# First output projection of a two-layer trunk: tokens stationary, seven block products for five of eleven row-tile pairs, result turned on TensorE

## The chip, the cores and the metric

The kernel runs on one core of a Trainium2 chip. The time is the device time of one execution in microseconds (us); of the kernel before, three runs gave 965.71, 966.10 and 966.26 us, median 966.1. A profile is one execution recorded by the hardware profiler. The engines are named as in the profile: PE is TensorE (matrix products; PEld its loads of stationary operands), DVE VectorE, ACT ScalarE, POOL GpSimd, SP the queue that issues the loads.

## The reference

The reference computes a decoder trunk in float32 for 256 tokens of width 1024. There are two layers; the first mixes tokens with a short convolution, the second with sparse attention. The part that the change touches is the first half-step feed-forward block and the start of the convolution mixer:

```python
def swiglu_ffn(x, w_in, w_out):
    gate, up = jnp.split(x @ w_in, 2, axis=-1)
    return (jax.nn.silu(gate) * up) @ w_out
...
    h = h + 0.5 * swiglu_ffn(rmsnorm(h, ffn1_norm[i]), ffn1_w_in[i], ffn1_w_out[i])
    hn = rmsnorm(h, mix_norm[i])
    h = h + short_conv_mixer(hn, conv_w_in[i], conv_w[i], conv_w_out[i])
```

The inner width is 2816, that is 22 tiles of 128 (`NF`). `short_conv_mixer` projects to three parts b, c and v, forms u = c v, runs a causal convolution of three taps over the tokens, multiplies with b and projects again.

## The kernel before, in words

**Numbers in two parts.** Each float32 operand is split into a high part in a shorter format (`F32R`) and the low rest. A product of tokens x and weights w is the sum of three: xh wh, xl wh and xh wl. ScalarE casts the high part of the weights (`Stream.high`, line 238), VectorE subtracts to get the low part (`Stream.low`, line 266). A weight unit is 128x1024 elements, eight tiles of 128x128, and half of a loaded chunk of 1 MB.

**Usual layout.** The residual h lies feature-major: eight tiles h[c] of 128 features x 256 tokens. Weights are stationary on TensorE, tokens move: [xh | xl] as 512 columns against wh, xh as 256 columns against wl (`half` and `a_pass`, lines 429 to 439). The order of the two passes alternates.

**The input projection** (`ffn_in`) makes the 22 inner tiles one after the other, two PSUM banks each; `ffn_evac` normalises by R, applies the gate and splits the result.

**The first output projection** (`out_proj`) makes eight output tiles c; each is a sum over 22 inner tiles, 44 matmuls. `out_evac` adds half of the result to h[c] and at once makes the next norm's operands for this tile: a high and a low part of g h[c] (`Norm.tile`, lines 379 and 383), and the squares on GpSimd. The norm factor R itself (`Norm.rows`) is a product with a matrix of ones, a square root and a reciprocal. It is not needed by the matmuls that follow, only by the evacuation of their results.

**The convolution's input projection** has eight groups f. Each takes three weight units (for c, v and b) into a pair of banks (`ocv`, a buffer of two) and one more bank, 24 matmuls of 512 and 24 of 256 columns. In group f=0, R is made between the sixth and the last k-tile (`conv_mid`). `conv_evac` then works through ScalarE, VectorE and GpSimd: sum of the two passes (lines 448, 449), product c v and its factor R squared on GpSimd (730, 731), taps (739 to 741), product with b (743) and a split (442, 443). Between its steps up to three weight units of later groups are prepared. Its output feeds the convolution's output projection, which starts with three output tiles over the first seven of the eight inputs.

**The last output projection** (`out_pairs`, matmuls at lines 1412 and 1464) is written differently. Tokens are stationary there (128 tokens, two halves) and weights move, 512 columns at a time. Inner tiles go in pairs p. A plain pair takes eight products of blocks; a block pair takes seven, in the manner of Strassen and Winograd, with sums of weight blocks that VectorE makes in place (line 167) and sums of token blocks made by `Pairs.add`. The set `PLAIN` says which pairs are plain. `add_pairs` puts the parts of the weights in an order: beside pair p, the second half of pair p+1 and the first parts of a block pair p+2. The parts of each go into eight PSUM accumulators, m[1] to m[8], from which sums give the four quarters of the result.

**What sets the order.** Every engine runs its instructions in the order in which the program writes them. There is no planner here, except a hand-written order for the attention, which is not touched. A wait of one instruction holds all behind it on its engine.

## Time and profile before

| What | Before |
|---|---|
| median of three runs | 966.1 us |
| span of the profiled execution | 963.8 us |
| first output projection (130.05 to 191.14) | 61.09 us |
| convolution's input projection (191.14 to 258.06) | 66.9 us |
| last output projection (903.47 to 960.56) | 57.1 us |

No time of the profiled execution as a whole is given beside its span; the span runs from its first to its last instruction. A row of the chain of waits has a start, a length, an engine, what it writes, its line and a count of merged instructions. A row of the timeline has the engine before the line; in square brackets stands how long the engine was idle before it and whose result ended that. A row of instruction groups has busy time and mean ns of one behind the bar.

### The profile page before, as it was taken

How to read it: one execution, taken by the hardware profiler on the slowest of the kernel's cores; microseconds unless marked ns; L12 is line 12 of the kernel's file. 1: busy time of each engine (PE TensorE's matmuls, PEld its weight loads, DVE VectorE, ACT ScalarE, POOL GpSimd, SP SyncE). 2: the span in 40 equal slices, each digit the busy share in tenths (PEclk: the TensorE clock that was granted, in tenths of full speed). 3: DMA queues.
4: the chain of work that ended last, by engine and by line, in shares of the span. 5: the costliest groups of instructions: out<-in, count | busy, mean ns of one | idle time of the engine just before them, and what ended most of it. 6: DMA issues, size and time to landing. Idle time of an engine off the chain costs nothing.

```text
span 963.8 us, 14683 instructions
## 1 busy us (share of the span) xinstructions
PE 958.1 (99%) x5609; PEld 839.4 (87%) x5609; DVE 755.0 (78%) x1213; ACT 581.9 (60%) x982; POOL 174.2 (18%) x266
## 2 busy tenths in 40 slices
PE   9999999999999999999999999999999999999998
PEld 7888888888888888888888888888987888888887
DVE  7987776678889888767659787866688788879896
ACT  7665653455556665644548787743479656656553
POOL 1000001144470100011321031001337350000002
PEclk9999999999999999999999999999999999999999
DMA  8665555546546975555635657554620364467362
GB/s 299 227 216 177 189 204 179 183 167 209 187 137 223 272 238 181 183 211 179 214 131 178 202 193 259 175 183 175 219 89 1 129 221 142 164 217 248 118 205 88
DMA packets 36423, 178.61 MB, mean 185 GB/s; under 512 B 3424, under 2 KB 7152, under 8 KB 18560
## 3 DMA queue, kind: packets, MB, share of 16 engines
q1 hardware_dynamic: 36352, 177.67, 54.1%
q8 instruction: 44, 0.72, 0.3%
q14 instruction: 27, 0.22, 0.1%
HBM read 175.52 MB, written 1.08 MB: 183 GB/s over the span
## 4 chain that ended last, share of the span: by engine, by line
PE 97%; DVE 1%; POOL 1%; DMA 0%; ACT 0%; issue 0%; SPq 0%; POOLq 0%
PE mm L430 55%; PE a L430 26%; PE a L1412 4%; PE mm L1412 2%; PE mm L1177 1%; PE a L1242 1%; PE a L812 1%; PE a L813 1%; PE a L814 1%; PE mm L655 1%; PE a L1222 1%; PE a L694 1%; DMA base<-in_first_dram 0%; POOL pr L1214 0%; DVE pr L1185 0%; PE a L925 0%
## 5 line engine op out<-in xcount | busy, mean ns | idle before, releaser
L266 DVE TENSOR_TENSOR wl<-ws,wh 128x1024 fp32r<-128x1024 f32 x263 | 326.5, 1252 | 68.4 <-ACT wh L238 42.8
L430 PE MATMUL mm<-xs,wh 128*128 128x512 f32 x1480 | 348.8, 390 | 0.0
L430 PEld LDWEIGHTS mm<-xs,wh 128*128 128x128 f32 x1480 | 273.6, 188 | 54.5 <-DVE xs L383 0.2
L238 ACT CAST wh<-ws 128x1024 fp32r<-128x1024 f32 x263 | 272.2, 1046 | 35.8 <-PE a L430 21.1
L430 PEld LDWEIGHTS mm<-xs,wl 128*128 128x128 f32 x1480 | 185.2, 192 | 4.2
L430 PE MATMUL mm<-xs,wl 128*128 128x256 f32 x1480 | 187.4, 283 | 0.0
L430 PE MATMUL a<-act,wh 128*128 128x512 f32 x608 | 141.7, 390 | 0.0
L430 PEld LDWEIGHTS a<-act,wh 128*128 128x128 f32 x608 | 113.0, 188 | 22.7
L449 DVE TENSOR_TENSOR t<-mm,t 128x512 f32<-128x512 f32 x95 | 65.2, 686 | 60.6 <-ACT t L448 59.9
L448 ACT COPY t<-mm 128x512 f32<-128x512 f32 x95 | 55.6, 585 | 73.7 <-PE mm L430 73.3
L430 PEld LDWEIGHTS a<-act,wl 128*128 128x128 f32 x608 | 75.7, 191 | 1.6
L430 PE MATMUL a<-act,wl 128*128 128x256 f32 x608 | 76.4, 283 | 0.0
L473 ACT ACTIVATE t<-t 128x256 f32<-128x256 f32 x88 | 36.8, 418 | 57.1 <-DVE t L460 57.0
L379 ACT ACTIVATE xs<-base 128x256 fp32r<-128x256 f32 x48 | 24.1, 506 | 77.0 <-DVE base L573 62.1
L460 DVE TENSOR_TENSOR t<-t,R 128x512 f32<-128x512 f32 (+1 forms) x88 | 57.3, 651 | 2.6
L442 ACT CAST act<-t 128x256 fp32r<-128x256 f32 x91 | 37.0, 407 | 28.8 <-DVE t L743 18.2
L397 POOL TENSOR_TENSOR t<-base 128x256 f32<-128x256 f32 x35 | 26.3, 751 | 134.7 <-DVE base L573 108.5
L443 DVE TENSOR_TENSOR act<-t,act 128x256 fp32r<-128x256 f32 x91 | 38.6, 424 | 5.7 <-ACT act L442 5.7
L383 DVE SCALAR_TENSOR_TENSOR xs<-base,xs 128x256 fp32r<-128x256 f32 x48 | 29.7, 622 | 16.9 <-ACT xs L379 16.8
L394 POOL TENSOR_TENSOR sq<-base 128x256 f32<-128x256 f32 x5 | 3.1, 615 | 219.4 <-DVE base L573 211.0
L474 DVE TENSOR_TENSOR t<-t,t 128x256 f32<-128x256 f32 x88 | 36.8, 418 | 4.6 <-ACT t L473 4.6
L1437 POOL TENSOR_TENSOR t<-t,base 128x512 f32<-128x512 f32 x4 | 5.9, 1478 | 163.6 <-ACT t L1435 163.6
(318 smaller groups left out, 1148.5 us busy)
## 6 DMA issues: line engine op xcount, KB each, us to landing
ws<-in_ffn_w_in_dram SPq DMA_DIRECT2D x69, 1024.0 KB, 5.0
ws<-in_ffn_w_out_dram SPq DMA_DIRECT2D x33, 1024.0 KB, 4.8
ws<-in_conv_w_in_dram SPq DMA_DIRECT2D x12, 1024.0 KB, 4.8
base<-in_ffn_w_in_dram SPq DMA_DIRECT2D x11, 1024.0 KB, 5.3
ws<-in_w_kv_dram SPq DMA_DIRECT2D x6, 1024.0 KB, 4.9
base<-in_ffn_w_pairs_dram SPq DMA_DIRECT2D x12, 512.0 KB, 4.7
kt<-in_ffn_w_in_dram SPq DMA_DIRECT2D x5, 1024.0 KB, 7.9
ws<-in_conv_w_out_dram SPq DMA_DIRECT2D x4, 1024.0 KB, 5.0
```

Of the source, the lines that this page charges most:

```text
L238: ac.copy(h, src)
L266: ve.tensor_tensor(out=l, in0=src, in1=h.bitcast(F32), op=ALU.subtract)
L383: ve.scalar_tensor_tensor(out=xs[c][:, T:], in0=h[c], scalar=gt[:, g + c:g + c + 1], in1=xs[c][:, :T].bitcast(F32), op0=ALU.mult, op1=ALU. ...
L430: pe.matmul(o if x == 0 else o[:, :T], u[x][:, q * P:(q + 1) * P], rhs if x == 0 else rhs[:, :T], start=start, stop=stop, skip_group_check ...
L442: ac.copy(dst[:, :T], src)
L443: ve.tensor_tensor(out=dst[:, T:], in0=src, in1=dst[:, :T].bitcast(F32), op=ALU.subtract)
L448: ac.copy(r, o[:, :, T:])
L449: ve.tensor_tensor(out=r, in0=o[:, :, :T], in1=r, op=ALU.add)
L460: ve.tensor_tensor(out=r, in0=r, in1=R[:, None, :].to_broadcast([P, n, T]), op=ALU.mult)
L473: ac.activation(s, r[:, 0], AF.Silu)
L474: ve.tensor_tensor(out=s, in0=s, in1=r[:, 1], op=ALU.mult)
L1412: pe.matmul(m[n], x, w, start=(count[n] == 0 and i == 0), stop=(count[n] == total[n] - 1 and i == 2), skip_group_check=True)
```

## The change

The first output projection now takes the form of the last one: tokens stationary, six plain pairs (0, 2, 5, 8, 9, 10) and five block pairs (`PLAIN1`). The weight array of the first layer is rearranged in memory for this, by the same function as that of the last. The layout of h must stay feature-major. So each of the four quarters of the result (`11`, `21`, `12`, `22`: token half, feature half), scaled by 0.5 R, is turned by four 128x128 transposes on TensorE, and VectorE adds the turned quarter to h (`turned`). The norm's operands are made by quarters (`piece`), and the squares by quarters of four tiles (`square4`). The factor 0.5 R is needed as a column per token; two small matmuls make it during the input projection (`half_rows`). Group f=0 of the convolution is cut in pieces (`conv_first`): k-tiles 0 to 3 of its first unit, then the turn of the last quarter, then k-tiles 0 to 3 of the other two units, then k-tiles 4 to 7 of all three. R is made in group f=1. A load of a small table moves from the end of the convolution into the input projection.

```diff
+    PLAIN1 = (0, 2, 5, 8, 9, 10)
...
-    W.add(A["ffn1_w_out"][0])
+    SEC1 = W.add_pairs(A["ffn1_w_pairs"], second_home, PLAIN1)
+    W.other.update({SEC1.c0 + p: (1, "kt", 0)[p % 3] for p in range(NP)})
...
+        def piece(self, c, at):
+            v = slice(T + at.start, T + at.stop)
+            for xs, g in self.sets:
+                ac.activation(xs[c][:, at], h[c][:, at], AF.Copy, scale=gt[:, g + c:g + c + 1])
+                ve.scalar_tensor_tensor(out=xs[c][:, v], in0=h[c][:, at], scalar=gt[:, g + c:g + c + 1], in1=xs[c][:, at].bitcast(F32),
+                                        op0=ALU.mult, op1=ALU.subtract)
+
+        def square4(self, x, tt):
+            s, to = act((P, 4, P), F32), self.sq[:, tt * P:(tt + 1) * P]
+            ac.activation(s, kt8[:, 4 * x:4 * x + 4, tt * P:(tt + 1) * P], AF.Square)
+            po.tensor_tensor(out=s[:, :2], in0=s[:, :2], in1=s[:, 2:], op=ALU.add)
...
+    def half_rows(R):
+        pb, r = bank(), sm([P, 2])
+        for tt in range(2):
+            pe.matmul(pb[:, tt:tt + 1], R[:1, tt * P:tt * P + P], ones[:1, :1], start=True, stop=True)
+        ac.activation(r, pb[:, :2], AF.Copy, scale=0.5)
+        return r
...
+        def turned(name, x, tt):
+            pb = bank([P, 4, P])
+            for a in range(4):
+                pe.transpose(pb[:, a], s[name][:, a * P:(a + 1) * P], ident)
+            v = kt8[:, 4 * x:4 * x + 4, tt * P:(tt + 1) * P]
+            ve.tensor_tensor(out=v, in0=pb, in1=v, op=ALU.add)
+
+        for p in range(last + 1):
+            B.product(p, *(2, 4 if p else 8) if p in S.plain else (1, 2))
+            B.prepare(p)
+            B.product(p, *(8, 4, 3) if p in S.plain else (3, 7, 6, 5, 4) if 0 < p < last else (1, 6, 7, 5, 2, 3, 4))
+        p = last + 1
+        B.product(p, 2, 4)
+        B.prepare(p)
+        s["s1"] = t2()
+        ac.copy(s["s1"], m[1])
+        B.product(p, 3, 8)
+        B.prepare(p + 1)
...
+        rest = range(p + 1, NP)
+        W.high()
+        W.low()
+        for q in rest:
+            B.product(q, 2)
+        add(s["11"], 2, s["11"], 0)
+        W.high()
+        W.low()
+        for q in rest:
+            B.product(q, 4)
+        add(s["21"], 4, s["21"], 1)
+        turned("11", 0, 0)
+        norm.square4(0, 0)
+        for n, q in enumerate(rest):
+            if n == len(rest) - 1:
+                turned("21", 0, 1)
+            B.product(q, 3)
+        for c in range(4):
+            norm.piece(c, slice(0, T))
+            if c == 1:
+                add(s["12"], 3, s["12"], 0)
+        for n, q in enumerate(rest):
+            if n == len(rest) - 1:
+                turned("12", 1, 0)
+            B.product(q, 8)
+        for c in range(4, 8):
+            norm.piece(c, slice(0, P))
+        norm.square4(0, 1)
+        add(s["22"], 8, s["22"], 1)
+        W.close(S)
+
+        def end():
+            turned("22", 1, 1)
+            for c in range(4, 8):
+                norm.piece(c, slice(P, T))
+            norm.square4(1, 0)
+            norm.square4(1, 1)
+            norm.ends()
...
+    def conv_first(end):
+        ob, ocv = bank(), bank2()
+        turn[0] = 0
+        o = [ocv[:, 0], ocv[:, 1], ob]
+        us = W.take(2)
+        a_pass([(o[0], us[0], xs, range(4))])
+        end()
+        a_pass([(o[1], us[1], xs, range(4))])
+        us += W.take(1)
+        a_pass([(o[2], us[2], xs, range(4))])
+        a_pass([(a, u, xs, range(4, 8)) for a, u in zip(o, us)])
+        W.done(3, False)
+        X["conv"] = conv_evac(0, ocv, ob, zs)
+        next(X["conv"])
+        W.pump()
...
-    for f in range(8):
+    for f in range(1, 8):
         ob, ocv = bank(), bank2()
-        a_group([ocv[:, 0], ocv[:, 1], ob], xs, mid=conv_mid if f == 0 else None, fresh=f < 2)
-        weave(conv_evac(f, ocv, ob, *box[0], zs), 1 if f == 7 else 3)
+        a_group([ocv[:, 0], ocv[:, 1], ob], xs, mid=conv_mid if f == 1 else None, fresh=f < 2)
+        if f == 1:
+            weave(X.pop("conv"), 2)
+        weave(conv_evac(f, ocv, ob, zs), 1 if f == 7 else 3)
```

The order of the instructions shows three places. The first is ScalarE of the changed kernel, at the end of f=0 of the convolution: L424 and L430 are the pieces and squares of the last quarter, `wh_1932` is the third weight unit of f=0, L482 the copy of f=0's first two banks, and the casts behind it are the three units of f=1.

```order
L424 ACTIVATE xs_1410<-base 128x128 [waits DVE_49]
L424 ACTIVATE xs_1411<-base 128x128
L424 ACTIVATE xs_1412<-base 128x128
L424 ACTIVATE xs_1413<-base 128x128
L430 ACTIVATE act_1911<-base 128x512
L430 ACTIVATE act_1916<-base 128x512
L243 CAST wh_1932<-ws_1745 128x1024 [waits DMAHW4_49,PE_49]
L482 COPY t_343_1968<-mm_1888 128x512 [waits PE_49,Activation_49]
L243 CAST wh_1971<-ws_1745 128x1024
L243 CAST wh_1977<-ws_1802 128x1024 [waits DMAHW5_49]
L243 CAST wh_1981<-ws_1802 128x1024
```

The units of f=0 and f=1 are cast here behind the pieces, where before they came ahead of the end of the projection.

The second place is VectorE around the reciprocal R. In the kernel before (L412 the reciprocal, L449 the sum of a group's banks, L266 a weight's low part, L443 the end of an evacuation), f=0's evacuation and then f=1's sum:

```order
L412 RECIPROCAL R_1948<-t_318_1946 128x256 [waits Activation_49]
L449 TENSOR_TENSOR t_321_1958<-mm_1900,t_321_1958 128x512 [waits Activation_49]
L266 TENSOR_TENSOR wl_1963<-ws_1859,wh_1961 128x1024 [waits DMAHW2_49,Activation_49]
L734 TENSOR_TENSOR t_325_1969<-a_1899,t_325_1969 128x256 [waits Activation_49]
L266 TENSOR_TENSOR wl_1977<-ws_1859,wh_1973 128x1024 [waits Activation_49]
L740 SCALAR_TENSOR_TENSOR t_329_1979<-u_1965,base,t_329_1979 128x256 [waits Activation_49]
L741 SCALAR_TENSOR_TENSOR t_329_1979<-u_1965,base,t_329_1979 128x256 [waits DVE_49]
L266 TENSOR_TENSOR wl_1985<-ws_1895,wh_1983 128x1024 [waits DMAHW3_49,Activation_49]
L743 TENSOR_TENSOR t_329_1979<-t_329_1979,t_325_1969 128x256 [waits DVE_49,Pool_49]
L443 TENSOR_TENSOR act_1988<-t_329_1979,act_1988 128x256 [waits Activation_49]
L449 TENSOR_TENSOR t_335_2041<-mm_1992,t_335_2041 128x512 [waits Activation_49]
```

And in the changed kernel, where the reciprocal stands in f=1 (L446 the reciprocal, L271 a low part, L477 the end of an evacuation, L483 the sum of f=1's banks):

```order
L446 RECIPROCAL R_2050<-t_362_2048 128x256 [waits Activation_49]
L901 TENSOR_TENSOR t_366_2064<-a_1887,t_366_2064 128x256 [waits PE_49,Activation_49]
L271 TENSOR_TENSOR wl_2072<-ws_1983,wh_2068 128x1024 [waits PE_49,Activation_49]
L907 SCALAR_TENSOR_TENSOR t_370_2074<-u_2060,base,t_370_2074 128x256 [waits Activation_49]
L908 SCALAR_TENSOR_TENSOR t_370_2074<-u_2060,base,t_370_2074 128x256 [waits DVE_49]
L271 TENSOR_TENSOR wl_2080<-ws_1993,wh_2078 128x1024 [waits DMAHW0_49,PE_49,Activation_49]
L910 TENSOR_TENSOR t_370_2074<-t_370_2074,t_366_2064 128x256 [waits DVE_49,Pool_49]
L477 TENSOR_TENSOR act_2083<-t_370_2074,act_2083 128x256 [waits Activation_49]
L271 TENSOR_TENSOR wl_2090<-ws_1993,wh_2086 128x1024 [waits PE_49,Activation_49]
L483 TENSOR_TENSOR t_377_2092<-mm_2002,t_377_2092 128x512 [waits Activation_49]
```

Evacuation 0 now follows f=1's group on TensorE, a third low part stands ahead of f=1's sum, and evacuation 1, further down, has no low parts between its steps.

The third place is VectorE at the end of the changed projection (L811 sums out of PSUM, L822 a turned quarter added to h, L425 the low pieces of the norm's operands):

```order
L811 SCALAR_TENSOR_TENSOR t_324_1779<-mm_1419,sm_403,t_324_1779 128x512 [waits Activation_49]
L271 TENSOR_TENSOR wl_1785<-ws_1708,wh_1783 128x1024 [waits DMAHW3_49,Activation_49]
L811 SCALAR_TENSOR_TENSOR t_321_1772<-a_1416,sm_403,t_321_1772 128x512 [waits PE_49]
L271 TENSOR_TENSOR wl_1804<-ws_1708,wh_1800 128x1024 [waits Activation_49]
L811 SCALAR_TENSOR_TENSOR t_323_1777<-a_1417,sm_403,t_323_1777 128x512 [waits PE_49]
L822 TENSOR_TENSOR base<-a_1819,base 128x4x128 [waits PE_49]
L822 TENSOR_TENSOR base<-a_1835,base 128x4x128 [waits PE_49]
L425 SCALAR_TENSOR_TENSOR xs_1406<-base,xs_1406 128x256 [waits Activation_49]
L425 SCALAR_TENSOR_TENSOR xs_1407<-base,xs_1407 128x256 [waits Activation_49]
L811 SCALAR_TENSOR_TENSOR t_322_1775<-a_1418,sm_403,t_322_1775 128x512 [waits PE_49]
```

None of these rows stands there before; the sums of the quarters, the lows of the convolution's weights and the pieces take turns in one queue.

More of the change, by code (lines that the diff above doesn't have):

```diff
@@ L247, in low @@
             half = self.half.pop(0)
-            if len(half) == 6 and not isinstance(half, list):
+            if len(half) == 7:
                 self.pair_low(*half)
@@ L357, in tables @@
     def tables():
-        sy.dma_start(small, A["small"])
         row = t2()
@@ L1370, in residual @@
         if f == 2:
-            pb, X["rows"] = bank(), sm([P, 2])
-            for tt in range(2):
-                pe.matmul(pb[:, tt:tt + 1], hid.R[:1, tt * P:tt * P + P], ones[:1, :1], start=True, stop=True)
-            ac.activation(X["rows"], pb[:, :2], AF.Copy, scale=0.5)
+            X["rows"] = half_rows(hid.R)
         if f in TURNS:
```

176 lines of the change are left out of this document (126 added, 50 removed).

## The prediction

> **What bounds the kernel now.** I read the page first, then the chain of waits, then single stretches.
>
> ```profile
> span 963.8 us, 14683 instructions
> PE 958.1 (99%) x5609; PEld 839.4 (87%) x5609; DVE 755.0 (78%) x1213; ACT 581.9 (60%) x982; POOL 174.2 (18%) x266
> PE 97%; DVE 1%; POOL 1%; DMA 0%; ACT 0%; issue 0%; SPq 0%; POOLq 0%
> ```
>
> TensorE is busy for 99% of the span and carries 97% of the chain: every TensorE microsecond saved counts, and so does every one in which TensorE is made to wait. The chain in order of time gives the stages:
>
> ```profile
> 24.46 105.59 PE mm L430 x608
> 130.05 61.09 PE a L430 x352
> ...
> 199.75 3.64 PE mm L430 x16
> ...
> 249.75 3.63 PE mm L430 x16
> ...
> 257.10 23.23 PE a L430 x136
> ...
> 575.50 0.87 PE a L895 x8
> ...
> 797.15 0.53 PE a L1373 x4
> 797.69 105.79 PE mm L430 x608
> 903.47 1.36 PE a L1412 x6
> ...
> 913.08 3.43 PE a L1412 x15
> ...
> 957.68 2.88 PE a L1464 x24
> ```
>
> The first output projection is the row at 130.05: 352 matmuls, 61.09 us, no gap. The same algebra that the change brings runs already as the last projection (L1412, L1464), from 903.47 to 960.56, also without a gap. At 199.75 ends f=0 of the convolution, with R made in it, and f=1 begins. The L1412 row of fifteen matmuls gives 3.43 / 15 = 0.2287 us for a matmul of 512 columns. Other engines have room on average, not everywhere:
>
> ```profile
> 903.47:957.68 54.21, 54.21 (x240) 44.51 (x239) 48.03 (x54) 29.93 (x36) 5.88 (x4) 1.00 0.43 141
> 130.05:191.14 61.09, 61.09 (x354) 54.14 (x353) 37.69 (x48) 27.69 (x33) 9.27 (x13) 1.00 0.54 190
> ```
>
> (Columns: stretch, length, then busy PE, PEld, DVE, ACT, POOL, clock, DMA.) VectorE works 48.03 of 54.21 us in the last projection and 37.69 of 61.09 in the first.
>
> **The change, TensorE's share.** The order of the new kernel has 249 matmuls of 512 columns in the section (six plain pairs of 24, five of 21): 249 x 0.2287 = 56.9 us for 61.09, a saving of 4.2. It adds sixteen 128x128 transposes; the row at 575.50 has eight in 0.87 us, so 1.75. The half-step column costs the row at 797.15, 0.53. Building the pair operands beside the input projection costs 105.79 - 105.59 = 0.2 by the two rows with 608 matmuls. Sum: -4.2 + 1.75 + 0.53 + 0.2 = **-1.7 us**, if nothing waits.
>
> **VectorE in the section.** The last projection shows the pace at which weights become ready:
>
> ```profile
> 908.09 2.36 DVE L172 TENSOR_TENSOR wl<-kt,wh 128x1024 fp32r<-128x1024 f32 x2 [0.53 <-ACT wh L161]
> 910.37 2.35 DVE L172 TENSOR_TENSOR wl<-ws,wh 128x1024 fp32r<-128x1024 f32 x2
> ...
> 914.38 2.67 DVE L167 TENSOR_TENSOR base<-base 128x1024 f32<-128x1024 f32 x3
> 917.52 2.36 DVE L172 TENSOR_TENSOR wl<-base,wh 128x1024 fp32r<-128x1024 f32 x2 [0.47 <-ACT wh L161]
> ...
> 947.51 2.35 DVE L172 TENSOR_TENSOR wl<-kt,wh 128x1024 fp32r<-128x1024 f32 x2
> 949.78 0.68 DVE L1429 SCALAR_TENSOR_TENSOR t<-mm,t 128x512 f32<-128x512 f32 x1
> base<-in_ffn_w_pairs_dram SPq DMA_DIRECT2D x12, 512.0 KB, 4.7
> ```
>
> VectorE runs there almost without a break: 1.15 us for a low part, 0.62 for a half one, 2.6 for the three subtractions (L167) of a block pair and 0.5 until ScalarE's cast is back. Count from the section's start. The lows of pair 1 are done at 910.45 - 903.47 = 6.98. The order of the new kernel prepares, beside each pair, the second half of the next one and the first one and a half parts of a block pair after it. Beside pair 1 these are three lows and a half one: 3.97, so 10.95. Beside pair 2, subtractions and two lows of block pair 3 and one and a half of block pair 4: 2.6 + 4 lows' worth less a half, 6.65, so 17.6 (the cast that waits for the chunk finds it landed, 4.7 and an issue behind 6.98). Beside pair 3, subtractions, a turn-around and two lows of pair 4: 5.4, so 23.0. Then 4.0 (27.0), 6.65 (33.65), 5.35 (39.0), 2.3 (41.3) and 2.3 (43.6). In the last projection block and plain pairs alternate up to 7 and 8; here two block pairs in a row come twice, 3, 4 and 6, 7, and eat the lead. Block pair 7 starts on TensorE at 35.67 (three plain pairs of 5.49, four block pairs of 4.80) and wants its third part at 37.5; its low is there at 37.95: a wait of 0.45, which goes into the tail's sum below and not beside it, because VectorE sets both. The last chunk's load is issued at 39.0, when the lows of pair 7 free its buffer; it lands 5.1 later (4.7 plus the first half's issue, 0.4), two casts of about 1.0 and one low of 1.2 behind them follow: 47.45.
>
> **The turned tail.** From 47.45 VectorE owes, before the last quarter can be turned: eight sums out of PSUM (0.68 to 0.75, 5.8 together), two convolution lows (2.4), three turned quarters added to h (0.69, 2.1), four full pieces of the low half (0.48, 1.95), four half pieces, and some 1.6 of waits for ScalarE (three turn-arounds of 0.5). Rows:
>
> ```profile
> L449 DVE TENSOR_TENSOR t<-mm,t 128x512 f32<-128x512 f32 x95 | 65.2, 686 | 60.6 <-ACT t L448 59.9
> L448 ACT COPY t<-mm 128x512 f32<-128x512 f32 x95 | 55.6, 585 | 73.7 <-PE mm L430 73.3
> L238 ACT CAST wh<-ws 128x1024 fp32r<-128x1024 f32 x263 | 272.2, 1046 | 35.8 <-PE a L430 21.1
> 193.06 0.48 DVE L383 SCALAR_TENSOR_TENSOR xs<-base,xs 128x256 fp32r<-128x256 f32 x1 [0.58 <-ACT xs L379]
> L521 DVE TENSOR_TENSOR t<-t,t 128x128 f32<-128x128 f32 x15 | 4.3, 286 | 0.2
> L1196 ACT ACTIVATE pr<-pr,sm 128x128 f32<-128x128 f32 x32 | 12.6, 403 | 0.0
> ```
>
> A half piece is not in the trace: 0.29 (L521) to 0.48 (L383) on VectorE, I take 0.30; on ScalarE 0.40 alone (L1196), 0.33 in a row. Sum 15.05, so the last turn may begin at 62.5 and ends at 63.05. TensorE by itself would be there at 56.9 + 4 x 0.44 + 1.39 (four of the convolution's k-tiles) = 60.05. TensorE's four turns stand in its queue between the last products, so that whatever a turn waits for holds the products behind it too. **Wait 3.0**, bounds 0.5 (VectorE's turn-arounds hidden) to 5 (one load late by its own 4.7).
>
> **The third convolution unit.** ScalarE's order puts the cast of f=0's third weight unit (wh_1932 in the order shown ahead) behind everything that the last quarter releases; the unit's source has long landed. From the end of the turn: VectorE's add 0.75, four half pieces 1.3, two squares 1.05 (585 ns each, overlapping), the cast 1.05: 4.15. TensorE has one k-half of the second unit, 1.39. It waits 2.75, and then 0.35 more for the low part (1.2 against four matmuls, 0.9): **3.1**, bounds 2.5 to 3.6. Next, the casts for f=1 stand behind the copy of f=0's banks, which are full four matmuls (0.91) before f=0 ends: 0.59 + 1.05 - 0.91 = **0.75**, bounds 0.3 and 1.2.
>
> **The convolution's chain.** R is now made in f=1's group, not f=0's: every evacuation needs it. Rows of the evacuations:
>
> ```profile
> 199.24 1.75 DVE L412 RECIPROCAL R<-t 128x256 f32<-128x256 f32 x1 [4.01 <-ACT t L410]
> ...
> 208.50 0.42 DVE L443 TENSOR_TENSOR act<-t,act 128x256 fp32r<-128x256 f32 x1 [0.47 <-ACT act L442]
> 208.98 0.69 DVE L449 TENSOR_TENSOR t<-mm,t 128x512 f32<-128x512 f32 x1
> ...
> 216.50 0.42 DVE L443 TENSOR_TENSOR act<-t,act 128x256 fp32r<-128x256 f32 x1 [0.47 <-ACT act L442]
> 216.99 0.69 DVE L449 TENSOR_TENSOR t<-mm,t 128x512 f32<-128x512 f32 x1
> ...
> 256.62 0.43 DVE L443 TENSOR_TENSOR act<-t,act 128x256 fp32r<-128x256 f32 x1 [0.47 <-ACT act L442]
> 257.76 0.69 DVE L449 TENSOR_TENSOR t<-mm,t 128x512 f32<-128x512 f32 x1 [0.71 <-ACT t L448]
> ...
> 263.44 0.42 DVE L443 TENSOR_TENSOR act<-t,act 128x256 fp32r<-128x256 f32 x1 [0.47 <-ACT act L442]
> ```
>
> One evacuation after the other takes 216.99 - 208.98 = 8.01 us, a TensorE group 8.33 (24 matmuls of each kind; 249.75 + 8.31 = 258.06 ends f=7). The chain has thus almost no reserve: f=6's result is written at 257.05 and the projection behind it wants it at 258.06 + 0.72, seven narrow matmuls later. Reserve 1.75. Now shift: a group later, +8.33; the third low and its cast stand between evacuations 0 and 1, +1.2; the sqrt for R is queued behind the cast of f=2's third unit, whose load waits for a buffer, +0.8; evacuation 1 has no lows woven in, 6.15 (257.76 to 263.44 and the next copy and sum) for 8.01, -1.85; less the reserve, -1.75. **7.0 us** (bounds 5.5, without the two delays, to 9, with lows in evacuation 1), part of it at f=3, which needs f=1's two banks. f=1's sum is ready 12.3 behind the end of its group (9.17 to the end of evacuation 0, as 208.92 - 199.75 is now, 1.2, 0.8, then copy and sum 1.1), f=2 ends at 8.33: of the 7.0, 4.0 stand at f=3, the rest at f=4 (its lows come out of evacuation 2) and at the projection.
>
> **Sum.** -1.7 + 3.0 + 3.1 + 0.75 + 7.0 = +12.15 on a span of 963.8: 975.95. The median 966.1 lies 2.3 above the profiled span; I keep that: **978.3 us**.
>
> **A rule weighed.** The clock stays whole in every window read, and the longest idle of TensorE that a row shows is this:
>
> ```profile
> PE a L348 <- DVE ones L328: 1.1, 1, 1.1
> ```
>
> The Trainium skill, "TensorE: Matmul & The Clock Gate", Part 1, says that an idle window of about 3.4 us halves the clock until a like time of work has passed. By that rule a gap longer than this would cost about 1.7 us more, an estimate (half of that time lost); by the row, which has no such gap, nothing is added.
>
> **Rivals.**
> A, the forecast: 978.3. Chance 0.72.
> B, the convolution does not pay: once evacuations lag behind TensorE they could run at the 6.15 of one without lows. Seven at 1.86 less are 13, more than the 7.0: only -1.7 + 6.85 = 5.15 stays, 971.3. For it: VectorE has idle time in the stage. Against: the lows stand in the order between the steps of an evacuation, as before. Chance 0.12.
> C, not slower: the queues do not bound at all, since the mechanism that would decide is cover: if ScalarE's casts and VectorE's sums come back inside the 8.78 us that f=0's pieces take and R one group later finds reserve, TensorE's count rules, 966.1 - 1.7 = 964.4. It decides where all waits together stay below 1.7. For it: the last projection runs gapless with VectorE at 48.03 of 54.21. Against: that one has no convolution behind it and is followed by nothing that needs all eight tiles. Chance 0.06.
> D, the clock falls behind a long gap: those at f=3 (4.0) and at the third unit (2.75, then 0.35) are the longest. If the fifteen matmuls behind each (3.43) ran at half rate, +3.4 each, 985.1. For it: such gaps are new. Against: the clock column never moves. Chance 0.10. The Trainium skill's rule named above would count f=3's gap alone and give 980.0.
> Loads starving the section is no rival: 11 MB in 57 us is what the old section draws (190 GB/s).
>
> **How the numbers follow.** A's own range is the sum of the lower and upper bounds, narrowed because they will not all fall one way: 974.5 to 982.5. To leave out no more than 2 in 10, the range takes in most of D and much of B: 972.0 to 984.0. A measurement here tells 0.2% (1.9 us) from no change. A, B and D are slower: 0.94. C splits about its 1.7 and takes what is left: 0.03 within, 0.03 faster.
>
> **What would show it.** Right: TensorE idle of about 2.8 us between the two thirds of f=0 with ScalarE's cast as releaser; about 0.7 before f=1; 4 us before f=3, released by VectorE; another wait at the convolution's output projection, on f=6; transposes late by 0.5 to 1 each; a section of about 60 us. Wrong: f=3 starts without a gap (B), or a section much longer than 61, which would mean that weights, not the tail, are late. A granted clock under 1 behind a gap is D.

## The result, and the profile after

The changed kernel takes 978.82 us (median of 4 runs, 978.18 to 978.86) against 966.18 (965.71 to 966.31, 4 runs) for the kernel before on the same chip: 1.3% slower, ratio 1.0131 with a 95% interval of 1.0117 to 1.0145. The forecast was 978.3. The sum came out this close partly by luck, because errors of both signs met in it; the runs below take it apart.

From the page of the changed kernel, the span, the busy times, and the shares of the chain of waits:

```profile
span 977.0 us, 14626 instructions
PE 960.4 (98%) x5526; PEld 835.2 (85%) x5526; DVE 779.1 (80%) x1263; ACT 596.8 (61%) x1011; POOL 165.1 (17%) x261
PE 86%; DVE 7%; ACT 3%; issue 2%; DMA 1%; POOL 0%; SPq 0%; ACTq 0%; DVEq 0%
```

TensorE had 83 matmuls fewer (5526 for 5609) and was busy 2.3 us longer, in part because some of them ran slowly. The chain that was 97% TensorE before is now 86%: VectorE (7%) and ScalarE (3%) have become links of it. The waits of TensorE, on its time line (start, length, engine, line, operation, tiles; in brackets the idle time ahead and its releaser):

```profile
169.18 0.50 PE L791 MATMUL mm<-wl,hm 128*128 128x512 f32 x1 [0.52 <-DVE wl L177]
184.46 0.66 PE L820 MATMUL a<-small,t 128*128 128x128 f32 x4 [1.14 <-DVE t L811]
...
193.87 0.66 PE L820 MATMUL a<-small,t 128*128 128x128 f32 x4 [0.38 <-DVE t L811]
...
198.59 2.08 PE L464 MATMUL a<-xs,wh 128*128 128x512 f32 x4 [2.66 <-ACT wh L243]
...
206.50 3.04 PE L464 MATMUL mm<-xs,wh 128*128 128x512 f32 x12 [0.77 <-ACT wh L243]
...
226.70 3.92 PE L464 MATMUL mm<-xs,wh 128*128 128x512 f32 x16 [2.96 <-DVE t L483]
...
238.00 1.21 PE L464 MATMUL a<-xs,wl 128*128 128x256 f32 x8 [0.79 <-DVE wl L271]
...
270.81 2.06 PE L464 MATMUL a<-act,wl 128*128 128x256 f32 x15 [0.43 <-ACT act L476]
...
294.74 1.88 PE L464 MATMUL mm<-xs,wh 128*128 128x512 f32 x7 [0.89 <-DVE xs L397]
```

All lie between 169 and 295 us, where the kernel before shows no wait of TensorE. They are pair 7's third part, the first and the last turn (with one of 0.34 between them the turns waited 1.9 in all), the third convolution unit, the start of f=1, f=3, f=4, the output projection (it waits for f=6's result) and the feed-forward block behind it. The four matmuls at 198.59 took 2.08 us where four such took 1.07 to 1.09 elsewhere. The time line by stretches shows why (stretch, length, busy PE, PEld, DVE, ACT, POOL, granted clock, DMA share, GB/s):

```profile
198.00:199.00 1.00, 0.41 (x1) 0.41 (x2) 0.43 (x1) 0.54 (x1) 0.92 (x3) 0.53 0.00 0
199.00:200.00 1.00, 1.00 (x3) 0.75 (x3) 1.00 (x1) 0.00 (x0) 1.00 (x1) 0.50 0.00 0
200.00:201.00 1.00, 1.00 (x5) 0.82 (x4) 0.03 (x1) 0.00 (x0) 0.92 (x2) 0.50 0.00 0
201.00:202.00 1.00, 1.00 (x9) 1.00 (x9) 0.00 (x0) 0.00 (x0) 0.85 (x3) 0.77 0.00 0
```

The granted clock was a half from 198.06, within the gap of 2.66 us, to 201.47. From the end of the gap that is (201.47 - 198.59) / 2 = 1.4 us lost at this place. Not all of it reaches the whole time: the four executions had mean granted clocks of 0.998, 0.995, 1.0 and 0.997 and spans of 977.0, 977.1, 976.4 and 977.0 us. The one at 1.0, without a slow stretch, was only 0.6 to 0.7 us shorter than the others. The likely reason is that waits behind the stretch come out shorter when TensorE is late; this was not followed up.

The rest of the stages' bounds, from TensorE's rows: the output projection, the feed-forward block behind it, and a later row of sixteen in that block. Before:

```profile
257.90 2.68 PE L430 MATMUL a<-act,wl 128*128 128x256 f32 x21
...
280.16 2.94 PE L430 MATMUL mm<-xs,wh 128*128 128x512 f32 x12
...
291.58 3.82 PE L430 MATMUL mm<-xs,wh 128*128 128x512 f32 x16
```

After:

```profile
269.49 0.88 PE L464 MATMUL a<-act,wl 128*128 128x256 f32 x6
...
292.55 1.29 PE L464 MATMUL mm<-xs,wh 128*128 128x512 f32 x5
...
305.10 3.82 PE L464 MATMUL mm<-xs,wh 128*128 128x512 f32 x16
```

With the section's start (130.05 and 131.24) and f=1's (199.75 and 206.50), stage by stage:

| stage | forecast | measured | how it is worked out |
|---|---|---|---|
| up to the section | +0.73 | +1.19 | 131.24 - 130.05; 0.44 of it lies in the first loads (the first long row starts at 24.90, not 24.46) |
| section and f=0 | +3.65 | +4.79 | to 205.73 (206.50 less the wait) in place of 199.75 |
| start of f=1 | +0.75 | +0.77 | the wait |
| f=1 to f=7 and the output projection | +7.0 | +5.64 | 86.05 for 80.41 us |
| start of the block behind it | 0 | +1.13 | 12.55 for 11.42 us |
| sum | +12.1 | +13.5 | span 977.0 for 963.8 is 13.2; the 0.3 between comes back behind 305.10 and is not assigned |

### The profile page after: what moved, and what is told of

The parts are those of the page before. It is cut to its first block, busy times and chain, and to the rows that moved or that the text cites. A ratio compares the mean times of both kernels' runs of the same rounds, so it can differ in the third digit from the quotient of the medians.

```text
span 977.0 us, 14626 instructions
## 1 busy us (share of the span) xinstructions
PE 960.4 (98%) x5526; PEld 835.2 (85%) x5526; DVE 779.1 (80%) x1263; ACT 596.8 (61%) x1011; POOL 165.1 (17%) x261
## 4 chain that ended last, share of the span: by engine, by line
PE 86%; DVE 7%; ACT 3%; issue 2%; DMA 1%; POOL 0%; SPq 0%; ACTq 0%; DVEq 0%
PE mm L464 51%; PE a L464 16%; PE a L1596 4%; DVE wl L271 2%; PE a L791 2%; PE mm L1596 2%; ACT wh L243 1%; PE mm L791 1%; PE mm L1364 1%; PE a L1429 1%; PE a L999 1%; PE a L1001 1%; PE a L1000 1%; DMA base<-in_first_dram 1%; PE a L1409 1%
## 5 line engine op out<-in xcount | busy, mean ns | idle before, releaser
L271 DVE TENSOR_TENSOR wl<-ws,wh 128x1024 fp32r<-128x1024 f32 x241 | 299.2, 1252 | 54.2 <-ACT wh L243 37.3
L243 ACT CAST wh<-ws 128x1024 fp32r<-128x1024 f32 x241 | 249.3, 1046 | 30.9 <-PE a L464 13.2
L483 DVE TENSOR_TENSOR t<-mm,t 128x512 f32<-128x512 f32 x95 | 65.2, 686 | 58.8 <-ACT t L482 58.0
L482 ACT COPY t<-mm 128x512 f32<-128x512 f32 x95 | 55.5, 584 | 75.2 <-PE mm L464 74.7
L464 PE MATMUL a<-act,wh 128*128 128x512 f32 x432 | 101.0, 390 | 0.0
L464 PEld LDWEIGHTS a<-act,wh 128*128 128x128 f32 x432 | 80.2, 188 | 16.2 <-DVE act L477 0.2
L464 PEld LDWEIGHTS a<-act,wl 128*128 128x128 f32 x432 | 54.0, 191 | 1.8 <-ACT act L476 0.6
L464 PE MATMUL a<-act,wl 128*128 128x256 f32 x432 | 54.8, 283 | 0.4 <-ACT act L476 0.4
L494 DVE TENSOR_TENSOR t<-t,R 128x256 f32<-128x256 f32 (+1 forms) x88 | 51.3, 583 | 2.6
L477 DVE TENSOR_TENSOR act<-t,act 128x256 fp32r<-128x256 f32 x86 | 37.9, 441 | 6.1 <-ACT act L476 6.1
L166 ACT CAST wh<-base 128x1024 fp32r<-128x1024 f32 x31 | 30.8, 1044 | 15.6 <-DVE base L172 8.3
L177 DVE TENSOR_TENSOR wl<-base,wh 128x1024 fp32r<-128x1024 f32 x31 | 36.5, 1218 | 1.7 <-ACT wh L166 1.7
L411 POOL TENSOR_TENSOR t<-base 128x256 f32<-128x256 f32 x28 | 21.6, 772 | 91.7 <-DVE base L614 89.1
```

Source lines behind the costliest of these rows:

```text
L177: ve.tensor_tensor(out=l, in0=src, in1=h.bitcast(F32), op=ALU.subtract)
L243: ac.copy(h, src)
L271: ve.tensor_tensor(out=l, in0=src, in1=h.bitcast(F32), op=ALU.subtract)
L464: pe.matmul(o if x == 0 else o[:, :T], u[x][:, q * P:(q + 1) * P], rhs if x == 0 else rhs[:, :T], start=start, stop=stop, skip_group_check ...
L477: ve.tensor_tensor(out=dst[:, T:], in0=src, in1=dst[:, :T].bitcast(F32), op=ALU.subtract)
L482: ac.copy(r, o[:, :, T:])
```

## The experiments

Names of the runs are those of the expectations. The kernel before was run beside each group and took 965.85 to 966.23 us.

| run | us | ratio to before, 95% interval |
|---|---|---|
| third_unit_first | 975.39 | 1.0098 (1.0083 to 1.0113) |
| r_at_start_of_f1 | 979.08 | 1.0139 (1.0122 to 1.0156) |
| r_late_alone | 972.78 | 1.0068 (1.0053 to 1.0083) |
| four_block_pairs | 977.92 | 1.0121 (1.0106 to 1.0137) |
| r_ahead_of_f2_cast | 977.24 | 1.0116 (1.0099 to 1.0133) |
| two_sums_earlier | 977.63 | 1.0121 (1.0106 to 1.0137) |
| conv_mended | 972.15 | 1.0065 (1.0050 to 1.0080) |
| conv_and_tail_mended | 970.04 | 1.0043 (1.0028 to 1.0058) |
| f1_sum_ahead_of_lows | 974.91 | 1.0097 (1.0082 to 1.0113) |
| all_mended | 968.93 | 1.0031 (1.0019 to 1.0042) |
| all_mended_four | 968.44 | 1.0026 (1.0017 to 1.0036) |
| all_mended_last | 968.51 | 1.0025 (1.0016 to 1.0034) |

Starts in different profiles are compared below from the first long row of TensorE, the feed-forward block, since that row itself starts between 24.12 and 25.11 with the first loads.

### The third unit's place

```diff
-        us = W.take(2)
+        us = W.take(3)
         a_pass([(o[0], us[0], xs, range(4))])
         end()
         a_pass([(o[1], us[1], xs, range(4))])
-        us += W.take(1)
```

> The changed kernel, but f=0's three weight units are all cast and split before its first matmul, so that the third stands ahead of the last quarter's work on ScalarE and VectorE. Theory (the gap between the two thirds of f=0 and the slow matmuls behind it come from that cast's place in ScalarE's order): the waits of 2.66 and 0.35 us and the stretch with a granted clock of 0.5 vanish; the last turn comes up to 1.2 us later, since one more low part stands ahead of it on VectorE. Against the changed kernel -2 to -3.5 us: 975.3 to 976.8. If the clock follows the gap, it stays at 1.00 there. Rival (VectorE's backlog sets both): the wait moves to the last turn in full, and the time stays within 0.8 us of 978.8.

975.39 us, 3.4 less than the changed kernel, as the theory had it. The gap between the thirds of f=0 and the slow stretch in it are gone, and the last turn started 0.2 us later (194.18 - 25.02 for 193.87 - 24.90), not 1.2. The cast's place in ScalarE's order was the cause; the unit's low part on VectorE moved with it, but the gap's releaser in the changed kernel is the cast. But a row of TensorE in this run also shows what the gain ran into:

```profile
224.19 6.76 PE L464 MATMUL mm<-xs,wh 128*128 128x512 f32 x16 [4.11 <-DVE t L483]
```

f=0 ended 3.8 us earlier (202.07 - 25.02 for 205.73 - 24.90), R did not come earlier by as much, and f=3 waited 4.11 in place of 2.96. And here the clock fell at f=3's gap: the sixteen matmuls took 6.76 us in place of 3.82. The waits that the changed kernel has behind f=3 (0.79, 0.43 and 0.89) do not occur in this run, so a part of what f=3 lost was saved there.

### What makes R late

```diff
+        if f == 1:
+            conv_mid()
-        a_group([ocv[:, 0], ocv[:, 1], ob], xs, mid=conv_mid if f == 1 else None, fresh=f < 2)
+        a_group([ocv[:, 0], ocv[:, 1], ob], xs, fresh=f < 2)
```

> The changed kernel, but the ones-product of the norm (from which R is made) goes to TensorE at the start of f=1's group, not after its first k-tiles. Theory (the convolution's chain is late by what R is late): R is ready 5 to 6 us earlier, so f=0's evacuation ends near 218.5 instead of 224.3; the waits at f=3 (2.96), f=4 (0.79) and the output projection (0.43) go, and so does most of the 1.3 us lost behind the output projection. Against the changed kernel -4 to -5.9: 973 to 975. Rival (the lows woven between the evacuation's steps, not R, set the chain's pace): the wait at f=3 shrinks, the later ones come back, and less than 2.5 us is gained. A second rival: the norm's parts are not ready at f=1's start, and TensorE waits there by as much as it saves later.

979.08 us: nothing gained. The theory fell, and the second rival was not it either, since TensorE did not wait for the norm's parts. The wait at f=3 was 3.18 us, and the clock fell there as well. ScalarE's rows of this run:

```profile
205.59 4.85 ACT L243 CAST wh<-ws 128x1024 fp32r<-128x1024 f32 x5
212.73 1.05 ACT L243 CAST wh<-ws 128x1024 fp32r<-128x1024 f32 x1 [2.28 <-DMA ws<-in_conv_w_in_dram]
...
215.09 0.47 ACT L444 ACTIVATE t<-a,epst 128x256 f32<-128x256 f32 x1
```

The ones-product had started at 205.77 and taken 0.40 us, almost nine microseconds ahead of the square root. Six casts stood in ScalarE's queue ahead of it, and the sixth, for f=2's third unit, waited 2.28 us for its load. The changed kernel has the same rows, 0.12 us earlier (212.61 for the sixth cast, 214.97 for the root). So with its product early, R is just as late by the order of ScalarE's work. That does not make the place on TensorE harmless. In the changed kernel the ones-product runs here:

```profile
213.95 0.40 PE L442 MATMUL a<-t,ones 128*128 128x256 f32 x2
```

It ended at 214.35, and the root started at 214.97. Two things held R to almost the same moment, TensorE's order and ScalarE's: to move the product alone gains nothing, as this run shows, and to free ScalarE's queue alone could have gained 0.6 us at most, an estimate from these two times; no run does that alone. The next run keeps the early product and puts the root ahead of that cast:

```diff
         next(X["conv"])
-        W.pump()
+        W.pump(5)
```

> The changed kernel with the ones-product at the start of f=1, as in r_at_start_of_f1, and only five units prepared ahead of it, so that the square root for R stands on ScalarE ahead of the cast of f=2's third unit, which waits for its load. Theory (R is late by its place in ScalarE's order, behind that cast, and not by TensorE's): the square root starts near 210.3 instead of 213.8 and R is there near 213.8 instead of 217.3; the wait at f=3 (3.2 in r_at_start_of_f1) falls under 0.5, the slow clock behind it does not come, and the waits at f=4 and behind the output projection shrink. Against r_at_start_of_f1 -4 to -6 us: 973 to 975. Rival (the chain from R on, GpSimd's products and the lows between its steps, sets f=3): R comes earlier and the wait shrinks by less than 1.5 us.

977.24 us, 1.8 less than r_at_start_of_f1. R came earlier (the root at 212.28, right behind its table load, 2.8 us earlier where 3.5 was expected), the wait at f=3 fell from 3.18 to 1.06, and the clock stayed whole there. The wait shrank by 2.1, more than the rival allowed, but it stayed above the theory's 0.5, the time gained less than its 4, and the waits at f=4 (0.78) and at the output projection (0.43) came back. VectorE's rows show what was next at f=3:

```profile
212.88 1.75 DVE L446 RECIPROCAL R<-t 128x256 f32<-128x256 f32 x1
...
221.26 0.42 DVE L477 TENSOR_TENSOR act<-t,act 128x256 fp32r<-128x256 f32 x1 [0.47 <-ACT act L476]
222.21 2.36 DVE L271 TENSOR_TENSOR wl<-ws,wh 128x1024 fp32r<-128x1024 f32 x2 [0.53 <-ACT wh L243]
224.49 0.69 DVE L483 TENSOR_TENSOR t<-mm,t 128x512 f32<-128x512 f32 x1
```

f=0's evacuation (L477) is done at 221.7, and f=1's sum (L483), for which f=3 waits, stands behind two more low parts. In the changed kernel one low part stood there. Ahead of them goes f=1's sum in the next run:

```diff
+        c = conv_evac(f, ocv, ob, zs)
         if f == 1:
-            weave(X.pop("conv"), 2)
-        weave(conv_evac(f, ocv, ob, zs), 1 if f == 7 else 3)
+            c0 = X.pop("conv")
+            next(c0)
+            W.pump(1)
+            next(c0)
+            next(c)
+            W.pump(1)
+            for _ in c0:
+                pass
+        weave(c, 1 if f == 7 else 3)
```

> r_ahead_of_f2_cast, and in addition f=1's copy and sum out of PSUM are issued between the steps of f=0's evacuation, ahead of two low parts for f=3 that stood in front of them there. Theory (once R is early, f=3 waits for f=1's sum, which stands behind those lows on VectorE and their casts on ScalarE): f=1's sum ends 5 to 9 us earlier, the wait at f=3 (1.06) goes, and the later ones at f=4 (0.78), at the output projection (0.43) and behind it (0.9), which are the same lateness handed on, go as well. Against r_ahead_of_f2_cast -2 to -3.2 us: 974 to 975.3; what is left of the convolution's 7.0 is then below 0.5. Rival (the lows that are put back are late themselves): TensorE waits in f=3 or f=4 for a low part by 1 us or more.

974.91 us, 2.3 less; of the 2.5 between the profiled executions 0.6 lies in the first loads (24.26 for 24.89). The wait at f=3 is gone. Those at f=4 (0.73), at the output projection (0.41) and behind it (0.90) stayed, against the expectation: they are not f=3's lateness handed on. From f=2 on one evacuation follows the other on VectorE, 8.0 us apart, and TensorE's groups 8.33, so a chain that is late gains only 0.3 a group.

### R late, and nothing else

The kernel before, with R made in f=1 as the changed kernel makes it:

```diff
-        a_group([ocv[:, 0], ocv[:, 1], ob], xs, mid=conv_mid if f == 0 else None, fresh=f < 2)
-        weave(conv_evac(f, ocv, ob, *box[0], zs), 1 if f == 7 else 3)
+        a_group([ocv[:, 0], ocv[:, 1], ob], xs, mid=conv_mid if f == 1 else None, fresh=f < 2)
+        if f == 0:
+            first = conv_evac(0, ocv, ob, zs)
+            next(first)
+            W.pump()
+            continue
+        if f == 1:
+            weave(first, 2)
+        weave(conv_evac(f, ocv, ob, zs), 1 if f == 7 else 3)
```

> The kernel before, with its first output projection as it was; only R is made in f=1's group instead of f=0's, and f=0's evacuation stops before the step that needs R until then, as in the changed kernel. Theory (R a group later costs by itself what the chain of the changed kernel shows: 2.96 + 0.79 + 0.43 of waits, and 1.3 behind the output projection): +4.5 to +6.5 us on the kernel before, 970.7 to 972.7. The forecast's own term was 7.0, 973.2. Rival (the evacuations catch up where the lows leave room, and the waits of the changed kernel come from the third unit and the tail): +0 to +2.

972.78 us, +6.6, just past the upper end of the theory. TensorE's waits:

```profile
193.26 2.37 PE L430 MATMUL mm<-xs,wh 128*128 128x512 f32 x9 [0.84 <-DVE xs L383]
...
219.64 5.53 PE L430 MATMUL mm<-xs,wh 128*128 128x512 f32 x16 [2.37 <-DVE t L449]
...
287.69 1.88 PE L430 MATMUL mm<-xs,wh 128*128 128x512 f32 x7 [0.95 <-DVE xs L383]
```

The first is this edit's own and not R's: without the ones-product, f=0 reads its last k-tiles earlier than the norm has them. The other two are R's, 3.3 us, and 5.53 - 3.82 = 1.7 more is the slow clock behind the first of them. Together 5.0 of the 6.4 by which the span grew (970.2 for 963.8), 0.84 for the first wait, 0.5 not assigned. The slow clock is not needed for that price: two of the four executions had a mean granted clock of 1.0 and spans of 971.0 and 970.9, the two at 0.998 had 970.2 and 971.2. So R a group later costs between 5 and 5.7 us by itself (6.55 less the first wait of 0.84), with the section as it was. Here the root did wait for the ones-product, with its table loaded and the casts for f=1 behind it:

```profile
207.91 0.47 ACT L410 ACTIVATE t<-a,epst 128x256 f32<-128x256 f32 x1 [3.78 <-PE a L408]
```

Here TensorE's order alone made R late; in the changed kernel both orders did, to within 0.6 us of each other.

### VectorE in the section

One more plain pair, one block pair less:

```diff
-    PLAIN1 = (0, 2, 5, 8, 9, 10)
+    PLAIN1 = (0, 2, 4, 6, 8, 9, 10)
```

> The changed kernel with four block pairs instead of five: one more pair by eight plain products. TensorE has three matmuls more (+0.69 us), VectorE 2.6 us of subtractions and about 1.2 of other work less in the section. Theory (the late turns are a backlog of VectorE): the waits of the turns (1.9 together) and of pair 7 (0.5) shrink to under 0.8 together, and the last turn ends earlier by 0.5 to 1.5 us; against the changed kernel -0.2 to -1.5. Rival (the waits are the turn-around between ScalarE and VectorE in the tail, whatever was prepared before): the waits stay, and the time is +0.5 to +0.9.

977.92 us, 0.9 less. Pair 7's wait is gone, the turns' waits fell from 1.9 to 1.0 (under 0.8 was expected), and the last turn started 1.3 us earlier (192.82 - 25.11) although TensorE had 0.7 us more to do. VectorE's backlog made up somewhat more than half of these waits; the rest stayed.

A part of that rest is order. In the changed kernel VectorE stood idle 1.68 us until the last cast and then did pair 10's low parts ahead of the first sums of the tail (L811):

```profile
176.48 2.36 DVE L177 TENSOR_TENSOR wl<-kt,wh 128x1024 fp32r<-128x1024 f32 x2 [1.68 <-ACT wh L166]
178.76 1.41 DVE L811 SCALAR_TENSOR_TENSOR t<-mm,t 128x512 f32<-128x512 f32 x2
```

Those two sums need only products that end with pair 7, but they were issued behind pair 8's, whose m[8] shares a two-bank tile with m[6].

```diff
+        s["u2"], s["u3"] = t2(), t2()
+        add(s["u2"], 6, s["s1"])
+        add(s["u3"], 7, s["u2"])
         B.product(p, 3, 8)
         B.prepare(p + 1)
-        s["u2"], s["u3"] = t2(), t2()
-        add(s["u2"], 6, s["s1"])
         scaled("11", s["s1"], 0)
-        add(s["u3"], 7, s["u2"])
```

> The changed kernel, but the two sums out of PSUM that need no plain pair (u2, u3) are issued ahead of the products 3 and 8 of the first of the last three pairs; in the changed kernel VectorE stood idle 2.5 us and then began them only when those products had ended. Theory (m[6] shares a two-bank tile with m[8], so the sum waits for products that it does not read, and VectorE's tail starts late by that): the first sum starts 4 to 6 us earlier, the waits of the turns (1.9) shrink under 1.0, and the last turn ends 0.5 to 1.5 us earlier; -0.4 to -1.5 on the changed kernel: 977.3 to 978.4. Rival (the low parts of the last pair move back by as much): TensorE waits for them instead, and the time is within 0.4 of 978.8 or above it.

977.63 us, 1.2 less, within the theory. The same rows now:

```profile
174.91 1.48 DVE L811 SCALAR_TENSOR_TENSOR t<-mm,t 128x512 f32<-128x512 f32 x2
176.46 2.36 DVE L177 TENSOR_TENSOR wl<-kt,wh 128x1024 fp32r<-128x1024 f32 x2
```

The sums fill the idle time, the low parts come no later, the turns wait 0.6 together, and the last turn starts 1.55 us earlier (192.48 - 25.06). What remains unseparated is whether the shared tile or merely VectorE's order held the sums: in four_block_pairs VectorE was idle for 2.5 us ahead of them with pair 8's products as the releaser, in the changed kernel, for which the expectation names those 2.5 us, the low parts hid that wait.

The profiles of both runs have a second slow stretch at f=3 (at gaps of 2.87 and 2.78 us; its sixteen matmuls took 5.31 and 5.54 us for 3.92 in the changed kernel), and they lack the changed kernel's waits at f=4 and at the output projection. So the 0.9 and 1.2 us are not the turns' alone.

### All mends together

R's ones-product after two of f=1's k-tiles, f=1's units cast ahead of the copy, the third unit first:

```diff
+        W.pump(3)
         W.done(3, False)
         X["conv"] = conv_evac(0, ocv, ob, zs)
         next(X["conv"])
-        W.pump()
+        W.pump(2)
...
-            a_pass([(o, u, xs, range(6)) for o, u in zip(parts, us)])
+            a_pass([(o, u, xs, range(at)) for o, u in zip(parts, us)])
```

> The changed kernel with three mends of the convolution together: f=0's third unit prepared first; f=1's three units cast ahead of the copy of f=0's banks; and R's ones-product after two of f=1's k-tiles, with the square root ahead of the cast of f=2's third unit. Theory (the losses behind the last turn are these waits and the slow clock that follows two of them): nothing waits from the last turn to the end of the convolution's output projection; what is left against the kernel before is the section itself, about +1.2 to +2.5: 967.5 to 969. Rival (VectorE has too little room in the stage): a new wait of 1 us or more in f=2, f=3 or at the output projection, 969.5 to 972.

972.15 us: 6.7 less than the changed kernel, but not the 967.5 to 969 of the theory; it is at the upper end of the rival's 969.5 to 972. In the profiled execution the waits named are gone and the clock is whole throughout, and new waits stand in f=1, above all for GpSimd's sums of squares:

```profile
PE a L442 <- POOL t L419: 1.3, 1, 1.3
...
PE mm L464 <- DVE xs L397: 1.0, 1, 1.0
...
PE a L464 <- DVE wl L271: 0.7, 1, 0.7
```

With the tail's order as well (the two sums, and the last sum ahead of the half pieces):

```diff
+        add(s["22"], 8, s["22"], 1)
         for c in range(4, 8):
             norm.piece(c, slice(0, P))
         norm.square4(0, 1)
-        add(s["22"], 8, s["22"], 1)
```

> conv_mended, with the two sums earlier as in two_sums_earlier, and the last sum of the turned tail ahead of the half pieces of the norm. Theory: the waits of the turns fall from 1.9 to under 0.8 and the last turn ends 1 to 1.8 us earlier than in conv_mended; 966 to 968. Rival (half pieces a sum later hold the convolution's second k-half): 0.7 lost between the thirds of f=0, no gain on conv_mended.

970.04 us: 2.1 less than conv_mended, somewhat more than the theory's 1 to 1.8; the turns wait 0.2 in all, and f=0 now ends 0.3 us ahead of the kernel before (199.18 - 24.20 for 199.75 - 24.46). The level was missed because conv_mended's was. Then the ones-product after five k-tiles, with f=1's sum ahead of the lows:

```diff
-        a_group([ocv[:, 0], ocv[:, 1], ob], xs, mid=conv_mid if f == 1 else None, fresh=f < 2, at=2)
+        a_group([ocv[:, 0], ocv[:, 1], ob], xs, mid=conv_mid if f == 1 else None, fresh=f < 2, at=5)
```

> conv_and_tail_mended, with the ones-product after five of f=1's k-tiles instead of two (GpSimd's sums of squares were not ready after two: 1.55 us of waits), and f=1's sum ahead of the lows as in f1_sum_ahead_of_lows. Theory: the waits of 1.3 + 0.3 (ones-product), 0.7 (a low part of f=1) and 1.0 (behind the output projection) go; 970.0 less 2.7 to 3.5 makes 966.5 to 967.3, and with what the last turn has gained, 965.5 at best: about the kernel before. Rival (the chain is still late behind f=1): 968 or more.

968.93 us, the rival's side again: the waits in f=1 went, and two came in f=3, for low parts that now stand behind the moved sum; the one behind the output projection stayed.

```profile
217.99 1.22 PE L464 MATMUL mm<-xs,wl 128*128 128x256 f32 x8 [0.35 <-DVE wl L271]
...
220.04 1.22 PE L464 MATMUL a<-xs,wl 128*128 128x256 f32 x8 [0.83 <-DVE wl L271]
...
284.76 1.89 PE L464 MATMUL mm<-xs,wh 128*128 128x512 f32 x7 [1.00 <-DVE xs L397]
```

The same with four block pairs (PLAIN1 as above):

> all_mended with four block pairs instead of five. TensorE +0.69 us, VectorE about 3.8 us less in the section. Theory: with the tail mended the waits left to remove are pair 7's 0.5 and the turns' 0.2, so the two cancel: within 0.5 us of all_mended. Rival (VectorE's backlog also delays what follows the last turn): 0.5 to 1.5 faster than all_mended.

968.44 us, 0.5 less, which is the line between the theory and the rival, and the two kernels' times overlap: once the tail is in order, the fifth block pair gains nothing, and whether it costs a little stays open. And, on all_mended_four, one low part of f=3 moved into a gap of VectorE (W.pump(2) in place of the first W.pump(1) of the sum's diff):

> all_mended_four, with one of the two low parts for f=3 moved from behind f=1's sum to ahead of it, into the 1.9 us in which VectorE there waits for GpSimd's products. Theory: the waits of 0.4 and 0.8 us that all_mended showed in f=3, for low parts that came too late, go, and the wait behind the output projection (1.0) stays, since the chain and TensorE both move: 968.4 less 1.2, 967.2, still above the kernel before (965.9). Rival (the cast waits for a weight buffer that f=1's last products free, and holds ScalarE's copy of f=1's banks behind it): no gain, 968.2 or more.

968.51 us, no gain; the rival has the time, though not for its reason. The waits in f=3 fell from 1.2 to 0.3, one of 0.2 appeared in f=5, and one of 0.55 for f=6's result at the output projection; the one behind it stayed (1.02). The best of these versions is still 0.25% above the kernel before.

## Why the prediction was right, and where not

**TensorE's share (-1.7).** Fifteen matmuls took 3.40 us, 0.2267 each, and the last turn stood where it was forecast, so the share holds; it was not measured by itself. The start of the section came 0.44 later by the first loads, which belong to no step.

**VectorE in the section and the tail (+3.0).** Pair 7 wanted its third part at 168.66, 37.42 behind the section's start, and had it at 37.94: forecast 37.5 and 37.95. The last turn ended at 194.28, 63.04 behind the start: forecast 63.05. Durations from the last projection's rows, laid in the order of the new kernel, were enough for this place. The waits themselves come to 0.52 + 1.86 = 2.4, not 3.0, and they were 1.14, none, 0.34 and 0.38 for the four turns and not 0.5 to 1 each; the other 0.6 lies in TensorE's own rows or around the gaps and was not separated. That the wait was there is right; that it had to be is not, since 1.55 us of it went with two sums moved.

**The third unit (+3.1).** 2.66 for 2.75 at the cast, with its cause shown by third_unit_first; the 0.35 for the low part vanished into the slow matmuls. The step lacked the clock: 1.4 us more in the profiled execution, so that the stage came to 4.79 for 3.65.

**f=1's casts (+0.75).** 0.77.

**The convolution's chain (+7.0).** This is the mis-sized term: f=3, f=4 and the projection waited 2.96 + 0.79 + 0.43 = 4.2, and the whole stage grew by 5.64; the 1.4 between lies in small pieces, some of them around the gaps, and was not separated. The terms that the prediction lists add up to 8.33 + 1.2 + 0.8 - 1.85 - 1.75 = 6.73, not 7.0. Two sizes behind it were too large. f=1's sum was ready at 226.64, 11.2 us behind f=1's end at 215.40, not 12.3, and evacuation 1 took 5.3, not 6.15 (VectorE's rows of the changed kernel; the sums L483 stand 5.28 apart):

```profile
215.47 1.75 DVE L446 RECIPROCAL R<-t 128x256 f32<-128x256 f32 x1 [0.56 <-ACT t L444]
...
225.96 0.68 DVE L483 TENSOR_TENSOR t<-mm,t 128x512 f32<-128x512 f32 x1
...
231.24 0.69 DVE L483 TENSOR_TENSOR t<-mm,t 128x512 f32<-128x512 f32 x1
```

Its first two terms stand: R a group later by its place on TensorE, and the root 0.8 later in ScalarE's queue; between the product's end and the root lay 214.97 - 214.35 = 0.6. What the prediction did not see, and r_at_start_of_f1 showed, is that this queue alone would have made R just as late.

**Behind the output projection (nothing in the sum).** The block behind it waited 0.89 and lost 1.13, because VectorE, late at the projection's start, carries its own sums and pieces through the whole projection: its first sum there starts 280.18 - 269.49 = 10.7 us behind the projection's start for 266.66 - 257.90 = 8.8 before, and the piece for which the block behind waits is ready 25.2 behind it for 23.3. r_late_alone has the same wait, 0.95, with nothing changed but R. The forecast had put all of the lateness at the projection.

**The rivals.** B (the lost time is caught up) would need evacuations of 6.15; from f=2 on they ran at 8.0. C fell with the waits that the time line shows. D was named with the right sign, in part: the clock fell at the third unit's gap, for 1.4 where D priced 3.4, and not at f=3's, the longer one. So A held with D's mechanism inside it, and the oversized chain (-1.4) stood against the clock, the projection's end and the first loads (+1.1, +1.1, +0.5). The places of the waits were forecast; that the total came within 0.5 us was luck.

## What to carry to other kernels

Where an operation is moved, ask on which engines' queues its result is held up, and look at all of them: R was late by its product's place on TensorE and by six casts, one of them waiting for a load, ahead of its root on ScalarE. The two ended within 0.6 us of each other, so moving the matmuls alone changed nothing. A saving in matmuls that needs other engines at a stage's end is worth what their reserve there is: 4.2 us of matmuls were saved here, the time grew by 12.6, and with everything mended that was found it was still 2.4 above the kernel before. Read a pace against a pace: a chain at 8.0 us behind groups of 8.33 hands any lateness on to the end of the stage and past it.

## What the hardware showed that was not expected

**The clock falls by frames, not by the length of a gap.** A gap of 2.66 us cost 1.4 us of slow matmuls, the next one of 2.96 none, and in other runs gaps of 2.37, 2.87 and 3.18 did. In every profile that has one before the last matmuls the slow stretch lasted 3.41 us or twice that, and in the three with two of them (r_at_start_of_f1, four_block_pairs, two_sums_earlier) they began 27.3 us, eight times 3.41, apart. If frames of 3.41 us are laid from the start of each slow stretch, these are TensorE's busy times in them (columns as above). The changed kernel, the frame that ends with the fall, the slow one, and the two that hold f=3's gap:

```profile
194.65:198.06 3.41, 1.28 (x7) 0.76 (x6) 1.83 (x5) 2.77 (x7) 0.82 (x2) 1.00 0.00 0
198.06:201.47 3.41, 2.88 (x9) 2.45 (x10) 1.46 (x1) 0.48 (x1) 3.17 (x5) 0.50 0.00 0
221.94:225.35 3.41, 1.80 (x8) 1.14 (x7) 2.42 (x4) 1.92 (x4) 0.00 (x0) 1.00 0.33 139
225.35:228.77 3.42, 2.07 (x9) 1.74 (x10) 1.65 (x4) 0.70 (x2) 1.97 (x3) 1.00 0.50 146
```

and third_unit_first, where two frames in a row were slow:

```profile
220.07:223.48 3.41, 0.01 (x1) 0.00 (x0) 2.42 (x5) 2.11 (x4) 0.00 (x0) 1.00 0.10 41
223.48:226.89 3.41, 2.70 (x6) 2.15 (x7) 1.61 (x5) 0.51 (x1) 2.09 (x4) 0.50 0.69 247
226.89:230.30 3.41, 3.41 (x9) 2.64 (x8) 2.52 (x5) 2.49 (x5) 0.73 (x1) 0.50 0.14 60
```

The profiles of all runs hold eleven slow stretches: each began behind a frame with TensorE busy for 1.29 us (38%) or less, and none behind a frame with 1.8 (53%) or more. A slow frame with 2.70 busy (79%) was followed by another, one with 2.88 (84%) was not. f=3's gap of 2.96 fell across two frames, each more than half busy. The Trainium skill, "TensorE: Matmul & The Clock Gate", Part 1, says that the window of about 3.4 us runs free; the trace agrees, with 3.41. That it takes a whole idle window of this length, as the prediction took from there, the traces contradict: frames up to 38% busy were enough. Going by that figure the prediction counted f=3's gap (4.0) alone and not the third unit's (2.75); in the changed kernel's profile the clock fell at the third unit's (2.66) and not at f=3's (2.96). Where the limits lie, for the fall between 38% and 53%, for the return between 79% and 84%, the traces bound and do not settle.

**GpSimd's additions beside VectorE's low parts.** In conv_mended the last sums of squares met three low parts; in third_unit_first they ran ahead of them. The same two instructions, there first and then in conv_mended:

```profile
201.12 0.46 POOL L435 TENSOR_TENSOR act<-act 128x128 f32<-128x128 f32 x1
201.66 0.46 POOL L436 TENSOR_TENSOR sq<-sq,act 128x128 f32<-128x128 f32 x1
```

```profile
201.83 1.32 POOL L435 TENSOR_TENSOR act<-act 128x128 f32<-128x128 f32 x1
203.23 1.32 POOL L436 TENSOR_TENSOR sq<-sq,act 128x128 f32<-128x128 f32 x1
```

0.46 became 1.32, and three low parts took 4.57 us in that run where five took 5.77 in the changed kernel. That is what made the ones-product wait in conv_mended: earlier low parts slowed the sums for which it waited. The Trainium skill, "SBUF — State Buffer", "SBUF: two separate sides", says that the two engines share a pair of ports under an exclusive lock, which counts against a VectorE instruction with two inputs in SBUF; the rows agree, since the additions took longer beside the low parts, which have two inputs, and not without them.
